# Moving cache-row copies, splitting the last factors by product and issuing three products before a norm

## The chip, the cores and the metric

The kernel runs on one core of a Trainium2 chip. The time is device microseconds (us) of one launch; the median of several runs is compared. A core has a matrix engine (PE, with PEld loading its weights), two elementwise engines (DVE and ACT), POOL, whose queue here issues DMAs and a few small operations, and SP, which issues DMAs only. All DMAs of the core run on the same 16 DMA engines: those that SP issues stand in queue q1, those that POOL issues in queue q0.

## The reference

One layer of a decoder for a prompt of 512 tokens and 8 samples of 4 tokens, 544 columns in all. What matters here is what follows the attention:

```python
y = jnp.concatenate([o_a, o_b], axis=-1) @ w_out          # h = h + y
up = rmsnorm(h, norm_ffn) @ w_up                          # 2048 -> 2 * 5504
conv = conv_b + sum(conv_w[j] * full[:, j:j + t] for j in range(3))
u, g = conv[..., :D_FF], conv[..., D_FF:]
h = h + (silu(g) * u) @ w_down
start = k_all.shape[1] - buf
return y, s_fin, k_all[:, start:], v_all[:, start:]       # the caches, shifted by 4 tokens
```

The new caches `k_s` and `v_s` are outputs: for each of the 8 samples, 1020 of the 1024 rows of 768 floats are the old rows, moved by four. That is 16 copies, 3060 KB each, from device memory to device memory. No other instruction reads or writes these rows.

## The kernel before

Activations lie feature by row, 128 features by 544 columns, each split into a high and a low part (`hi`, `lo`) so that three matmuls make one product in higher precision. A weight tile is loaded (`raw`), its high part made by ACT (`whi`, L190) and its low part by DVE (`wlo`, L191); three of each are kept.

The stages that matter, in order:

- **Output projection** (`for ot in range(KD)`, 16 output tiles). Each tile's `h` is loaded by POOL, gets the product added by DVE (L904), is stored by POOL to `hscr` (L905), squared into `acc2`, and scaled by ACT in place (L913), which waits until that store has read it.
- **Factors.** The up stage multiplies by a scheme of seven products on 2x2 blocks (in place of eight). Two tiles of `h` make one row pair `i` of four blocks b11, b12, b21, b22, from which `factors()` makes seven right-hand factors B11, B21, B22, T1 to T4, each split by `parts()` into `vh` (ACT, L875) and `vl` (DVE, L876). The first four pairs are done inside the output projection, the last four (4 to 7) when the projection has ended, pair by pair, over scratch tiles `ts` and `tu`.
- **Up stage**: 43 column pairs (`class Pair`). Pair `f` runs seven products `p1, p5, p6, p2, p7, p3, p4` of 24 matmuls each. Some of its weights are sums of two blocks: SP loads the first and POOL adds the second with an accumulating DMA (L957). Its result `a` is stored by POOL to `adr[f]` (L1085), save for three kept pairs (`KEPT`, 39 to 41), which stay on chip. After each odd `f` below 32, POOL also issues one cache copy (L1088).
- **Down stage.** First 16 products with the three kept pairs alone (24 matmuls and a 192 KB weight load each), then group 0 and group 1 of 16 pairs each and group 2 with the rest. SP fetches the pairs back from `adr` (`ar`, L1108), two buffers at a time, along with the weights (L829).

A scheduler sets the order on each engine when the program is built, from priorities (`tc.high_priority`); `tc.keep_in_program_order` pins a copy to its place among POOL's instructions. Each engine then runs its list in that order and waits on semaphores; an instruction that waits holds all that stand behind it. POOL's DMAs signal eight semaphores in turn (DMASW0 to 7). Tiles of a closed pool give their memory to the next pool, whose first user waits for the last users of the old one: so the first fetch `ar<-adr[0]` also waits for the store of the last pair, `adr[42]`.

Of the kernel before, what the change touches and what calls it, by code (L numbers as in the profile page):

```python
# [9 lines left out]
F32 = mybir.dt.float32  # L10
# [113 lines left out]
def _build(tc, nc, es, xT, st_gla, ck, cv, conv_in, vecs, w_in, w_gu, w_out, w_up, w_dn,  # L124
# [172 lines left out]
    def gps():  # L297
        return pg.tile([P, 2, 512], F32, tag="g", name="g")
# [573 lines left out]
    def parts(i, v, n, src):  # L872

        H, L = vh[i][:, v:v + n], vl[i][:, v:v + n]
        nc.scalar.activation(H, src, AF.Copy)  # L875
        nc.vector.tensor_sub(L, src, H.bitcast(F32))  # L876

    def factors(some, X, pool):
        for i in some:
            vh[i] = pool.tile([P, NV, HT], F32R, name=f"vh{i}")  # L880
            vl[i] = pool.tile([P, NV, HT], F32R, name=f"vl{i}")
            parts(i, B11, 1, X[i][:, 0, :HT].unsqueeze(1))
        for i in some:
            b11, b12, b21, b22 = X[i][:, 0, :HT], X[i][:, 0, HT:], X[i][:, 1, :HT], X[i][:, 1, HT:]
            t = HX.tile([P, 2, HT], F32, tag="ts", name="ts", bufs=1)
            u = HX.tile([P, 2, HT], F32, tag="tu", name="tu", bufs=1)
            nc.vector.tensor_sub(t[:, 0], b11, b12)
            nc.vector.scalar_tensor_tensor(t[:, 1], t[:, 0], -1.0, b22, op0=OP.mult, op1=OP.subtract)
            parts(i, T1, 2, t)
            nc.vector.tensor_sub(u[:, 0], b22, b12)  # L890
            nc.vector.scalar_tensor_tensor(u[:, 1], t[:, 1], -1.0, b21, op0=OP.mult, op1=OP.subtract)
            parts(i, T3, 2, u)
            parts(i, B21, 2, X[i][:, 1].rearrange("p (a c) -> p a c", a=2))

    X = {}
    for ot in range(KD):
        ps = gps()
        gemm(ps, [wpart(w_out, order[:8], ot * P), wpart(w_out, order[8:], ot * P)], og)
        i, j = divmod(ot, 2)
        if j == 0:  # L900
            hp = HX.tile([P, 2, NT], F32, tag="h", name="h", bufs=KD // 2 + 1 - AHEAD)
        ht = hp[:, j]
        nc.gpsimd.dma_start(ht, xT[ot * P:(ot + 1) * P, :])
        nc.vector.tensor_add(hv(ht), hv(ht), ps[:, :, :HT])  # L904
        nc.gpsimd.dma_start(hscr[ot], ht)  # L905
        if ot == 0:
            nc.scalar.activation(acc2, ht, AF.Square)
        else:
            sq = htmp("sq")
            nc.scalar.activation(sq, ht, AF.Square)  # L910
            nc.vector.tensor_add(acc2, acc2, sq)
        X[i] = hp
        nc.scalar.activation(ht, ht, AF.Copy, scale=vec[:, V_FFN + ot:V_FFN + ot + 1])  # L913
        if j == 1 and i < AHEAD:
            factors([i], X, VA)
# [27 lines left out]
    class Pair:  # L943
# [41 lines left out]
        def p2(self):  # L985
            with ahead():
                self.a12 = self.load((0, 1))
                A = wsplit(self.a12)
                nc.vector.tensor_add(self.s, self.s, self.a12)
            y = self.g[:, 1]  # L990
            product(y, A, B21)
            self.Fu, self.Fg = [FP.tile([P, FW], F32, tag="F", name="F", bufs=2) for _ in range(2)]
            for s, F in enumerate((self.Fu, self.Fg)):
                nc.gpsimd.memset(F[:, 0:2], 0.0)
                nc.scalar.activation(F[:, 2 + TP:].rearrange("p (b s) -> p b s", s=2 + TS)[:, :, 0:2],
                                     self.ci[:, s].rearrange("p (b r) -> p b r", r=2), AF.Copy, scale=(1.0, -1.0)[s])
            nc.vector.tensor_add(self.Fu[:, 2:2 + HT], y[:, :HT], self.V)

        def p7(self):
            with ahead():  # L1000
                A = wsplit(self.load((0, 0), (1, 0)))
            product(self.b0, A, T3, False)
            U3 = tmp("V")
            nc.scalar.activation(U3, self.b0[:, :HT], AF.Copy)
            second(self.Fg, self.z, U3)
            R = slice(2 + HT, FW)
            nc.vector.scalar_tensor_tensor(self.Fg[:, R], self.Fg[:, R], -1.0, rstdF[:, R], op0=OP.mult, op1=OP.mult)
# [30 lines left out]

    pairs = [Pair(f) for f in range(KF)]
    pairs[0].p1()  # L1040
    rms_stat(acc2, rstd, htmp)
    closed(hx_p)
    g0_p, G0 = opened(name="g0", bufs=NKEPT, side="right")
# [17 lines left out]
    for f, pr in enumerate(pairs):  # L1061
        if f % 4 == 0:
            n = min(4, KF - f)
            ci = FP.tile([P, 2, 4, 2 * NB], F32, tag="ci", name="ci", bufs=2)
            co = FP.tile([P, 2, 4, 2 + 2 * NB], F32, tag="co", name="co", bufs=2)
            nc.gpsimd.dma_start(ci[:, :, :n, :], ci_v[:, :, f:f + n, :])
        pr.ci, pr.co = ci[:, :, f % 4, :], co[:, :, f % 4, :]
        pr.p5()
        pr.p6()
        pr.p2()  # L1070
        pr.p7()
        if f + 1 < KF:
            pairs[f + 1].p1()
        pr.p3()
        pr.p4()
        cu, cg = pr.conv()
        nc.scalar.activation(cg[:, :FW - 2], cg[:, :FW - 2], AF.Silu)
        a = FP.tile([P, NT], F32, tag="a", name="a", bufs=1)
        nc.vector.tensor_mul(a[:, :TP], cu[:, :TP], cg[:, :TP])
        nc.vector.tensor_mul(a[:, TP:].rearrange("p (b t) -> p b t", t=TS), sv(cu), sv(cg))  # L1080
        if f in KEPT:
            kept[f] = (G0.tile([P, NT], F32R, tag="dh", name="dh"), G0.tile([P, NT], F32R, tag="dl", name="dl"))
            split(kept[f][0], kept[f][1], a)
        else:
            nc.gpsimd.dma_start(adr[f], a)  # L1085
        if f % 2 == 1 and f < 4 * NB:
            b, (src, dst) = f // 4, ((ck, k_s), (cv, v_s))[f // 2 % 2]
            tc.keep_in_program_order(nc.gpsimd.dma_start(dst[b, 0:PAST - TS, :], src[b, TS:PAST, :]))  # L1088
        if f % 4 == 3 or f == KF - 1:
            f4 = f - f % 4  # L1090
            nc.gpsimd.dma_start(co_v[:, :, f4:f + 1, :], co[:, :, :f + 1 - f4, :])
# [65 lines left out]
    for gi, ks in enumerate(groups):  # L1157
        A = {}
        with tc.high_priority(offset=min(2000, tc.cur_priority - P0)):
            for k in ks:  # L1160
                A[k] = A1[k] if k in A1 else fetch(k, where[k])
        if gi < len(groups) - 1:
            for ot in range(KD):
                ps = gps()
                gemm(ps, [wpart(w_dn, ks[i:i + 8], ot * P) for i in range(0, len(ks), 8)], A)
                nc.vector.tensor_add(hv(h[ot]), hv(h[ot]), ps[:, :, :HT])
                if gi == 0:
                    x = W3.tile([P, NT], F32, tag="hr", name="hr", bufs=1)
                    nc.sync.dma_start(x, hscr[ot])
                    nc.vector.tensor_add(h[ot], h[ot], x)  # L1170
# [113 lines left out]
```

## Time and profile before

| | us |
|---|---|
| median of 3 runs (2546.86 to 2550.66) | 2549.17 |
| the profiled execution, its own time | 2555.3 |
| its span | 2553.5 |
| PE busy (97% of the span) | 2483.1 |
| DVE busy | 1625.9 |
| ACT busy | 1063.8 |
| POOL busy | 459.4 |

The profile's page gives the busy time of each engine, the span in slices, the DMA queues, the chain of work that ended last, and groups of instructions by line. Here the chain is mostly PE, so what counts is where PE had to wait. Times in the views are counted from the start of the span. The output projection lies at about 888 to 1071 us, the up stage at 1071 to 2012, the kept products at 2012 to 2060, the groups of the down stage after that.

### The profile page before, as it was taken

How to read it: one execution, taken by the hardware profiler on the slowest of the kernel's cores; microseconds unless marked ns; L12 is line 12 of the kernel's file. 1: busy time of each engine (PE TensorE's matmuls, PEld its weight loads, DVE VectorE, ACT ScalarE, POOL GpSimd, SP SyncE). 2: the span in 40 equal slices, each digit the busy share in tenths (PEclk: the TensorE clock that was granted, in tenths of full speed). 3: DMA queues.
4: the chain of work that ended last, by engine and by line, in shares of the span. 5: the costliest groups of instructions: out<-in, count | busy, mean ns of one | idle time of the engine just before them, and what ended most of it. 6: DMA issues, size and time to landing. Idle time of an engine off the chain costs nothing.

```text
span 2553.5 us, 47085 instructions
## 1 busy us (share of the span) xinstructions
PE 2483.1 (97%) x19479; PEld 2384.3 (93%) x19479; DVE 1625.9 (64%) x2432; ACT 1063.8 (42%) x1820; POOL 459.4 (18%) x592
## 2 busy tenths in 40 slices
PE   7999999999999999999999999999999999999997
PEld 6988887899999899999999999999999999999997
DVE  7777754267776844477777878787788643342244
ACT  5344555133334443355554545454555531131142
POOL 4333424210001320021212222222121000000001
PEclk9999999999999999999999999999999999999999
DMA  7777734532222273579999999999998474453332
GB/s 202 204 198 210 191 93 131 158 94 68 75 76 76 68 204 116 127 156 279 240 274 236 267 249 261 254 269 248 239 194 180 117 223 115 112 150 91 86 97 71
DMA packets 581591, 427.72 MB, mean 168 GB/s; under 512 B 18976, under 2 KB 553728, under 8 KB 580608
## 3 DMA queue, kind: packets, MB, share of 16 engines
q1 hardware_dynamic: 462144, 248.31, 35.4%
q0 software_dynamic: 115200, 171.02, 29.4%
q10 hardware_dynamic: 4032, 5.38, 0.6%
q8 instruction: 153, 2.51, 0.4%
q14 instruction: 62, 0.51, 0.1%
HBM read 397.40 MB, written 77.37 MB: 186 GB/s over the span
## 4 chain that ended last, share of the span: by engine, by line
PE 76%; DMA 13%; DVE 5%; issue 2%; ACT 1%; POOL 0%; DVEq 0%; ACTq 0%; SPq 0%; POOLq 0%
PE g L225 43%; PE b L931 15%; PE g L931 10%; DMA raw<-in_w_up_dram 9%; DMA q<-qscr 4%; PE s L660 1%; PE v L507 1%; PE s L555 1%; PE s L542 1%; DVE wlo L191 1%; ACT whi L190 1%; DVE pr L411 1%; PE s L778 1%; PE s L781 0%; DVE h L1215 0%
## 5 line engine op out<-in xcount | busy, mean ns | idle before, releaser
L190 ACT ACTIVATE whi<-raw 128x1024 fp32r<-128x1024 f32 (+1 forms) x345 | 355.5, 1031 | 641.8 <-PE g L225 476.1
L191 DVE TENSOR_TENSOR wlo<-raw,whi 128x1024 fp32r<-128x1024 f32 (+1 forms) x341 | 408.9, 1200 | 285.2 <-ACT whi L190 280.8
L225 PE MATMUL g<-ah,wlo 128*128 128x272 f32 x2048 | 442.6, 294 | 0.0
L225 PE MATMUL g<-al,whi 128*128 128x272 f32 x2048 | 440.5, 293 | 0.0
L225 PE MATMUL g<-ah,whi 128*128 128x272 f32 x2048 | 437.3, 292 | 2.9 <-ACT whi L190 2.0
L931 PE MATMUL b<-vh,whi 128*128 128x272 f32 x1376 | 397.6, 290 | 16.4 <-ACT whi L190 15.6
L931 PE MATMUL b<-vl,whi 128*128 128x272 f32 x1376 | 397.0, 289 | 0.0
L931 PE MATMUL b<-vh,wlo 128*128 128x272 f32 x1376 | 390.6, 289 | 0.0
L225 PEld LDWEIGHTS g<-ah,whi 128*128 128x128 f32 x2048 | 325.0, 189 | 17.4 <-issue 12.9
L225 PEld LDWEIGHTS g<-ah,wlo 128*128 128x128 f32 x2048 | 326.2, 189 | 11.5 <-issue 10.1
L225 PEld LDWEIGHTS g<-al,whi 128*128 128x128 f32 x2048 | 325.4, 189 | 12.2 <-issue 10.3
L931 PE MATMUL g<-vh,whi 128*128 128x272 f32 x1032 | 298.1, 289 | 2.9 <-ACT vh L875 2.9
L931 PE MATMUL g<-vl,whi 128*128 128x272 f32 x1032 | 299.1, 290 | 1.3 <-DVE vl L876 1.3
L931 PE MATMUL g<-vh,wlo 128*128 128x272 f32 x1032 | 296.7, 287 | 0.0
L931 PEld LDWEIGHTS b<-vh,whi 128*128 128x128 f32 x1376 | 260.9, 190 | 19.3 <-ACT whi L190 18.2
L225 PE MATMUL g<-dh,whi 128*128 128x272 f32 x1248 | 258.3, 289 | 4.3 <-ACT whi L190 2.3
L931 PEld LDWEIGHTS b<-vl,whi 128*128 128x128 f32 x1376 | 260.5, 189 | 0.0
L225 PE MATMUL g<-dh,wlo 128*128 128x272 f32 x1248 | 258.9, 289 | 0.0
L225 PE MATMUL g<-dl,whi 128*128 128x272 f32 x1248 | 258.5, 289 | 0.0
L931 PEld LDWEIGHTS b<-vh,wlo 128*128 128x128 f32 x1376 | 258.2, 189 | 0.0
L190 ACT ACTIVATE whi<-rs 128x1024 fp32r<-128x1024 f32 x129 | 136.7, 1059 | 258.3 <-PE g L931 151.0
L225 PEld LDWEIGHTS g<-dh,whi 128*128 128x128 f32 x1248 | 196.5, 189 | 5.2 <-ACT whi L190 2.9
(340 smaller groups left out, 4116.8 us busy)
## 6 DMA issues: line engine op xcount, KB each, us to landing
raw<-in_w_up_dram SPq DMA_DIRECT2D x129, 512.0 KB, 7.5
raw<-in_w_in_dram SPq DMA_DIRECT2D x96, 512.0 KB, 4.3
raw<-in_w_dn_dram SPq DMA_DIRECT2D x64, 512.0 KB, 4.0
out_k_s_dram<-in_ck_dram POOLq DMA_DIRECT2D x8, 3060.0 KB, 16.9
out_v_s_dram<-in_cv_dram POOLq DMA_DIRECT2D x8, 3060.0 KB, 17.1
ra<-in_w_up_dram SPq DMA_DIRECT2D x43, 512.0 KB, 7.8
rs<-in_w_up_dram SPq DMA_DIRECT2D x43, 512.0 KB, 3.9
rs<-in_w_up_dram POOLq DMA_DIRECT2D x43, 512.0 KB, 11.4
```

The costliest lines, as they stand in the source:

```text
L190: nc.scalar.activation(hi, src, AF.Copy)
L191: eng.tensor_sub(lo, src, hi.bitcast(F32))
L225: nc.tensor.matmul(ps[:, s, :HT], a, b[:, s * HT:(s + 1) * HT], start=(i == 0 and n == 0), stop=(i == len(todo) - 1 and n == 2))
L411: nc.vector.tensor_mul(pr, kt[:, 4:5, :].broadcast_to([P, TS, QC]), q5[:, 1:5, :])
L507: nc.tensor.matmul(psv[32 * m:32 * m + 32, :QC], lhs, rhs, start=(kt == 0), stop=(kt == 5), tile_position=(0, 32 * m))
L542: nc.tensor.matmul(psc[:, :n], q[r, qi * P:(qi + 1) * P], k[r, :n], start=True, stop=True)
L555: nc.tensor.matmul(psc[r, :P], vt[:, j * P + 64 * e:j * P + 64 * e + 64], t[:, j * P:(j + 1) * P], start=(j == 0), stop=(j == qi))
L660: nc.tensor.matmul(ps[:, c * P:(c + 1) * P], KS[:, c * P:(c + 1) * P], Q[:, :, c * 64:(c + 1) * 64], start=True, stop=True)
L778: nc.tensor.matmul(po[:, c * P:(c + 1) * P], V[:, c, e * P:(e + 1) * P], ST[:, 2 * c + e, :], start=True, stop=(c == 0))
L931: nc.tensor.matmul(b[:, :HT], a_[:, i, :], x_[i][:, v, :], start=(first and i == 0 and n == 0), stop=(i == 7 and n == 2), skip_group_check ...
```

## The change

Three things. The sixteen copies leave the up stage: a list `kept_rows` holds them, and `keep_rows()` issues one each time it is called, in the output projection when `ot % 3 == 1` (5 copies) and in groups 0 and 1 of the down stage at every second tile (the other 11). `factors()` works in place of the blocks of `h` instead of `ts` and `tu`, and for the last four pairs it goes product by product over all four, with parts of one block each. `pairs[0].p5()` and `p6()` stand ahead of the norm (`rms_stat`) beside `p1()`; and the addition `s += a12` moves from `p2` to `p7`.

```diff
     def factors(some, X, pool):
+        b = {}
         for i in some:
...
-            parts(i, B11, 1, X[i][:, 0, :HT].unsqueeze(1))
+            b[i] = X[i].rearrange("p a (b c) -> p (a b) c", c=HT)
+        late = len(some) > 1
         for i in some:
-            t = HX.tile([P, 2, HT], F32, tag="ts", name="ts", bufs=1)
...
+            parts(i, B11, 1, b[i][:, 0:1])
+        for i in some:
+            nc.vector.tensor_sub(b[i][:, 0], b[i][:, 0], b[i][:, 1])
+            parts(i, T1, 1, b[i][:, 0:1])
+        for i in some:
+            nc.vector.scalar_tensor_tensor(b[i][:, 0], b[i][:, 0], -1.0, b[i][:, 3], op0=OP.mult, op1=OP.subtract)
+            parts(i, T2, 1, b[i][:, 0:1])
...
+    kept_rows = [(b, src, dst) for b in range(NB) for src, dst in ((ck, k_s), (cv, v_s))]
+    def keep_rows():
+        if kept_rows:
+            b, src, dst = kept_rows.pop(0)
+            tc.keep_in_program_order(nc.gpsimd.dma_start(dst[b, 0:PAST - TS, :], src[b, TS:PAST, :]))
     for ot in range(KD):
+        if ot % 3 == 1:
+            keep_rows()
...
     pairs[0].p1()
+    pairs[0].p5()
+    pairs[0].p6()
     rms_stat(acc2, rstd, htmp)
...
-        if f % 2 == 1 and f < 4 * NB:
-            b, (src, dst) = f // 4, ((ck, k_s), (cv, v_s))[f // 2 % 2]
-            tc.keep_in_program_order(nc.gpsimd.dma_start(dst[b, 0:PAST - TS, :], src[b, TS:PAST, :]))
...
                 nc.vector.tensor_add(hv(h[ot]), hv(h[ot]), ps[:, :, :HT])
+                if (gi * KD + ot) % 2 == 1:
+                    keep_rows()
```

How the built programs stand: POOL, from the last pairs of the up stage to the end; before, then after. `adr_9233<-a` is the store of the last pair (42), `co` the last convolution rows.

```order
L994 MEMSET F 128x2 [waits DVE_49,Activation_49] x2
L957 DMA raw<-in_w_up_dram 128x8x128 [waits DMASW4_49,DMAHW6_49,DMASW2_49,Activation_49]
L994 MEMSET F 128x2 [waits DVE_49,Activation_49] x2
L1091 DMA out_conv_out_dram<-co 256x1x54 [waits DMASW5_49,Activation_49]
L1085 DMA adr_9233<-a 128x544 [waits DVE_49]
L1215 TENSOR_TENSOR h<-h,rstd 128x272 [waits DVE_49,DMASW0_49,PE_49,Activation_49]
```

```order
L1116 DMA out_conv_out_dram<-co 256x1x54 [waits DMASW2_49,Activation_49]
L916 DMA out_v_s_dram<-in_cv_dram 48x16320
L916 DMA out_k_s_dram<-in_ck_dram 48x16320 [waits DMASW4_49]
L916 DMA out_v_s_dram<-in_cv_dram 48x16320 [waits DMASW5_49]
L916 DMA out_k_s_dram<-in_ck_dram 48x16320 [waits DMASW6_49]
L916 DMA out_v_s_dram<-in_cv_dram 48x16320
L916 DMA out_k_s_dram<-in_ck_dram 48x16320 [waits DMASW0_49]
L916 DMA out_v_s_dram<-in_cv_dram 48x16320 [waits DMASW1_49]
L916 DMA out_k_s_dram<-in_ck_dram 48x16320 [waits DMASW2_49]
L916 DMA out_v_s_dram<-in_cv_dram 48x16320 [waits DMASW3_49]
L916 DMA out_k_s_dram<-in_ck_dram 48x16320 [waits DMASW4_49]
L916 DMA out_v_s_dram<-in_cv_dram 48x16320 [waits DMASW5_49]
L1113 DMA adr_9233<-a 128x544 [waits DMASW6_49,DVE_49]
```

The 11 copies of the down stage stand in one row between the last convolution rows and the last pair's store, which now stands behind them; between them there is no other instruction.

SP at the start of the down stage, before, then after: loads of the kept products' weights (128x3x128), and the first fetches `ar`.

```order
L829 DMA raw<-in_w_dn_dram 128x3x128 [waits DMAHW7_49,DVE_49]
L1108 DMA ar<-adr_9191 128x544 [waits DMASW5_49,DMASW6_49,DMASW1_49,DMASW7_49,PE_49,Pool_49]
L1108 DMA ar<-adr_9192 128x544
L829 DMA raw<-in_w_dn_dram 128x3x128 [waits DMAHW0_49,DVE_49]
L1108 DMA ar<-adr_9193 128x544 [waits DMAHW3_49,DVE_49]
L829 DMA raw<-in_w_dn_dram 128x3x128 [waits DMAHW1_49,DVE_49]
```

```order
L829 DMA raw<-in_w_dn_dram 128x3x128 [waits DMAHW1_49,DVE_49]
L1133 DMA ar<-adr_9191 128x544 [waits DMASW4_49,DMASW2_49,DMASW6_49,PE_49,Pool_49]
L1133 DMA ar<-adr_9192 128x544
L829 DMA raw<-in_w_dn_dram 128x3x128 [waits DMAHW2_49,DVE_49]
L829 DMA raw<-in_w_dn_dram 128x3x128 [waits DMAHW3_49,DVE_49]
L829 DMA raw<-in_w_dn_dram 128x3x128 [waits DMAHW4_49,DVE_49]
```

In both, the first `ar` waits for the store of `adr_9233` (its semaphore is DMASW6); ahead of it SP has 11 of the 16 weight loads before and 13 after, and the other loads stand behind it.

DVE after the output projection's last tile, the first factors of the late pairs (`vl_11184` and so on are four tiles, one for each pair), before, then after:

```order
L876 TENSOR_TENSOR vl_11185<-ts,vh_11184 128x544 [waits Activation_49]
L876 TENSOR_TENSOR vl_11185<-tu,vh_11184 128x544 [waits Activation_49]
L876 TENSOR_TENSOR vl_11185<-h,vh_11184 128x544 [waits Activation_49]
L876 TENSOR_TENSOR vl_11189<-h,vh_11188 128x544 [waits Activation_49]
L876 TENSOR_TENSOR vl_11193<-h,vh_11192 128x544 [waits Activation_49]
L887 TENSOR_TENSOR ts<-h 128x272 [waits DVE_49]
```

```order
L876 TENSOR_TENSOR vl_11190<-h,vh_11189 128x272 [waits Activation_49]
L889 TENSOR_TENSOR h<-h 128x272 [waits DVE_49]
L876 TENSOR_TENSOR vl_11192<-h,vh_11191 128x272 [waits Activation_49]
L889 TENSOR_TENSOR h<-h 128x272 [waits DVE_49]
L876 TENSOR_TENSOR vl_11194<-h,vh_11193 128x272 [waits Activation_49]
L889 TENSOR_TENSOR h<-h 128x272 [waits DVE_49]
```

Parts of 544 columns became parts of 272, and the pairs alternate; no order within a pair is forced by a scratch tile.

## Rows read from the trace of the kernel before

**Rows 1.** Windows: length, busy time (instructions) PE, PEld, DVE, ACT, POOL, clock, DMA share, GB/s.

```profile
888.00:1071.00 183.00, 183.00 (x1460) 183.00 (x1459) 79.63 (x107) 62.21 (x80) 20.17 (x33) 1.00 0.51 143
1071.00:1096.50 25.50, 18.36 (x104) 15.75 (x104) 23.28 (x42) 17.07 (x32) 4.21 (x7) 0.80 0.51 121
...
1265.00:1855.00 590.00, 574.56 (x4542) 572.14 (x4543) 456.81 (x625) 293.20 (x517) 123.28 (x162) 0.99 1.07 254
```

**Rows 2.** Waits of PE at 1265 to 1855: total us, times, longest.

```profile
PE b L931 <- ACT whi L190: 15.6, 12, 2.9
```

**Rows 3.** Chain that ended last, up stage: start us, us, what; one such piece each pair.

```profile
1096.74 8.64 PE b L931 x69
...
1243.84 8.64 PE b L931 x69
...
1265.88 8.95 PE b L931 x69
...
1854.42 8.64 PE b L931 x69
...
1980.50 8.64 PE b L931 x69
```

**Rows 4.** DMA queues at 1237 to 1243, inside one copy: packets, MB, share.

```profile
q0 software_dynamic: 32, 2.09, 97.8%
q1 hardware_dynamic: 31, 0.02, 0.9%
```

**Rows 5.** The load of ra that SP issued at 1232.4, just before that copy's packets.

```profile
DMA to landing us min/median/max: 19.1/19.1/19.1
```

**Rows 6.** The loads of ra at 1890 to 1940, with no copy near.

```profile
DMA to landing us min/median/max: 7.5/8.9/10.4
```

**Rows 7.** The accumulating load rs that POOL issued at 1230.7, just behind that copy.

```profile
DMA to landing us min/median/max: 21.1/21.1/21.1
```

**Rows 8.** The page's DMA issues: the same load over the whole run.

```profile
rs<-in_w_up_dram POOLq DMA_DIRECT2D x43, 512.0 KB, 11.4
```

**Rows 9.** DVE in order of time, late factors: start us, us, instruction.

```profile
1072.37 1.23 DVE L191 TENSOR_TENSOR wlo<-rs,whi 128x1024 fp32r<-128x1024 f32 x1
...
1080.57 1.22 DVE L191 TENSOR_TENSOR wlo<-raw,whi 128x1024 fp32r<-128x1024 f32 x1
1081.71 0.72 DVE L876 TENSOR_TENSOR vl<-h,vh 128x544 fp32r<-128x544 f32 x1
1082.34 0.43 DVE L888 SCALAR_TENSOR_TENSOR ts<-ts,h 128x272 f32<-128x272 f32 x1
1082.70 0.43 DVE L169 SCALAR_TENSOR_TENSOR rs<-v,rs 128x272 f32<-128x272 f32 x1
...
1091.61 0.72 DVE L876 TENSOR_TENSOR vl<-tu,vh 128x544 fp32r<-128x544 f32 x1
```

**Rows 10.** PE in order of time: first matmul of pair 0 and first of its p7.

```profile
1071.33 0.28 PE L931 MATMUL b<-vh,whi 128*128 128x272 f32 x1
...
1096.58 0.29 PE L931 MATMUL b<-vh,whi 128*128 128x272 f32 x1
```

**Rows 11.** POOL in order of time at the end of the up stage.

```profile
2014.94 0.72 POOL L1091 DMA_DIRECT2D out_conv_out_dram<-co  x1 [13.65 <-ACT co L1029]
2020.70 0.60 POOL L1085 DMA_DIRECT2D adr<-a  x1 [5.04 <-DVE a L1080]
```

**Rows 12.** SP's queue in order of time, same place.

```profile
1997.16 26.80 SPq L829 DMA_DIRECT2D raw<-in_w_dn_dram  x11
2024.18 0.82 SPq L1108 DMA_DIRECT2D ar<-adr  x2
```

**Rows 13.** DMA issues at 1997 to 2024: KB each, us to landing.

```profile
adr<-a POOLq DMA_DIRECT2D x1, 272.0 KB, 2.6
```

**Rows 14.** Chain that ended last, 1995 to 2065: kept products, then group 0.

```profile
2011.81 10.56 PE g L225 x84
...
2059.83 5.17 PE g L225 x27
```

More of the change, by code (lines that the diff above doesn't have):

```diff
@@ L881, in factors @@
             vl[i] = pool.tile([P, NV, HT], F32R, name=f"vl{i}")
-            parts(i, B11, 1, X[i][:, 0, :HT].unsqueeze(1))
+            b[i] = X[i].rearrange("p a (b c) -> p (a b) c", c=HT)
+        late = len(some) > 1
         for i in some:
-            b11, b12, b21, b22 = X[i][:, 0, :HT], X[i][:, 0, HT:], X[i][:, 1, :HT], X[i][:, 1, HT:]
-            t = HX.tile([P, 2, HT], F32, tag="ts", name="ts", bufs=1)
[L886 to L893, printed above, removed]
+            parts(i, B11, 1, b[i][:, 0:1])
[5 more added lines that the diff above has]
+            parts(i, T2, 1, b[i][:, 0:1])
+        for i in some:
+            parts(i, B21, 1 if late else 2, b[i][:, 2:3] if late else b[i][:, 2:4])
+        for i in some:
+            nc.vector.tensor_sub(b[i][:, 1], b[i][:, 3], b[i][:, 1])
+            if late:
+                parts(i, T3, 1, b[i][:, 1:2])
+        if late:
+            for i in some:
+                parts(i, B22, 1, b[i][:, 3:4])
+        for i in some:
+            nc.vector.scalar_tensor_tensor(b[i][:, 2], b[i][:, 0], -1.0, b[i][:, 2], op0=OP.mult, op1=OP.subtract)
+            if late:
+                parts(i, T4, 1, b[i][:, 2:3])
+            else:
+                parts(i, T3, 2, b[i][:, 1:3])
+    kept_rows = [(b, src, dst) for b in range(NB) for src, dst in ((ck, k_s), (cv, v_s))]
[3 more added lines that the diff above has]
+            tc.keep_in_program_order(nc.gpsimd.dma_start(dst[b, 0:PAST - TS, :], src[b, TS:PAST, :]))
     X = {}
     for ot in range(KD):
+        if ot % 3 == 1:
+            keep_rows()
         ps = gps()
@@ L988, in p2 @@
                 A = wsplit(self.a12)
-                nc.vector.tensor_add(self.s, self.s, self.a12)
             y = self.g[:, 1]
@@ L1000, in p7 @@
             with ahead():
+                nc.vector.tensor_add(self.s, self.s, self.a12)
                 A = wsplit(self.load((0, 0), (1, 0)))
@@ L1067, in _build @@
         pr.ci, pr.co = ci[:, :, f % 4, :], co[:, :, f % 4, :]
-        pr.p5()
-        pr.p6()
+        if f:
+            pr.p5()
+            pr.p6()
         pr.p2()
```

## The prediction

> **What bounds the kernel now.** I read the windows by stage first. In the output projection PE is busy for the whole 183.00 us with the DMA engines at 0.51 [rows 1]: nothing is to be won there, and there is room for transfers. Two stretches lose time, and a third is short. (1) At the start of the up stage, 1071 to 1096.5, PE is busy 18.36 of 25.50 us at a granted clock of 0.80. (2) At 1265 to 1855 PE is busy 574.56 of 590 us, at clock 0.99, with the DMA engines full (1.07). (3) Between the up stage and group 0, 2011.81 to 2059.83, lie 48 us for the kept products [rows 14]. The waits of stretch 2 are of one kind, PE for a weight that ACT has yet to split, 15.6 us in 12 waits [rows 2]; the weight is late because its load is. The chain shows the price per pair: from 1096.74 to 1243.84 seven pairs take 21.01 us each, and so do the six from 1854.42 to 1980.50 [rows 3].
>
> What a cache copy does to the loads is seen inside one. From 1237 to 1243 POOL's queue q0 had 32 packets with 2.09 MB, 97.8% of the 16 engines, and SP's queue q1 31 packets with 0.02 MB [rows 4]. So the queues took turns packet by packet, but a copy's packet has 65 KB and lasts 0.978 x 6 x 16 / 32 = 2.93 us, a load's some 0.5 KB. SP's load of `ra`, waiting all that time, took 19.1 us [rows 5] against 7.5 to 10.4 without a copy [rows 6]. While a copy runs, loads stand still.
>
> **The change part by part.**
>
> *Copies out of the up stage.* From 1243.84 to 1854.42 are 28 pairs (the one from 1243.84 to 1265.88 and 27 more) in 610.58 us; at 21.01 they would take 588.3. The copies cost 22.2 us [rows 3]. Pairs without copies, at both ends, lose nothing, and the accumulating loads were there all the same; so I take all of it, **-22**. Bounds: -11 (half of it, if the accumulating loads alone run late in some pairs) and -23.
>
> *Five copies in the output projection.* They stand 36 us apart (three tiles), each behind a store of `h`; the next store comes a tile (12 us) later. One copy holds the loads for some 9 us (3 packets per engine x 2.93, since 3060 KB in 65 KB packets are 48, on 16 engines). SP loads a weight three tiles ahead of its use, with PE at 100% and the engines at 0.51 [rows 1]. This cover hides them: **0**. Without it a copy would cost what it cost in the up stage, 22.2 / 16 = 1.4 us, so 0 to +7.
>
> *Factors and three products ahead of the norm.* DVE sets this stretch: from 1072.37 on it has hardly a gap, and its last late factor starts at 1091.61 [rows 9]. PE starts pair 0 at 1071.33 and its p7 at 1096.58 [rows 10]; the 25.25 us hold four products, 96 matmuls of 0.125 (21.01 / 168), 12.0 us, and four matmuls of the norm. The parts of 544 cost 0.63 us each on DVE (1081.71 to 1082.34), those of 272 0.36 (1082.34 to 1082.70) [rows 9], so splitting them costs, and after the change more weights stand in between. DVE's list from `wlo<-rs` to the last late factor is now: 28 low parts and 16 differences of 272 at 0.36, 15.8 us; four weights at 1.14 (1080.57 to 1081.71), 4.6; the addition to `rs`, 1.1; `acc`, 0.6; three steps of the norm, 1.1. That is 23.2 us, to 1095.6, later than the 1092.3 of before. But the last four parts (T4) are wanted last; those of T2, which p6 needs, end at some 1093, and PE has its 96 matmuls out then, about 3 us sooner, after which pair 1's p1 waits for its weight. I take **-2**. Bounds: -12 (all that is lost there: 25.25 - 12.0 - 1.5), if the products really follow each other without a wait, and +3, if DVE's longer list is what decides.
>
> *Eleven copies at the end of the up stage.* In the source they are spread over two groups of the down stage. In the order they are not: POOL has no other work there, a copy depends on nothing, so POOL issues all 11 in one row as soon as the last convolution rows are out, at 2014.94 + 0.7 [rows 11], and the store of the last pair, issued at 2020.70 before, stands behind them. Copies 9 to 11 and the store wait for a semaphore of one eight DMAs earlier, which ends well before their turn. The 11 take 33 packets per engine x 2.93 = 97 us (or 34.5 MB at the 2.09 MB in 6 us: 99) [rows 4]. Starting about 2 us after the issue, at 2017.7, they end near 2115, and the store lands 2.6 us later [rows 13], at 2117 against 2023.3. Who waits for it: SP's first fetch `ar`, which needs the memory of the closed pools; it came at 2024.18, right after that landing [rows 12, 11, 13]. Behind that fetch stand all later weight loads and fetches on SP. PE has what is loaded: some seven of the 16 kept products (3.0 us each, 84 matmuls in 10.56 us) [rows 14], until about 2033, since the loads in the queue stand still as in [rows 4, 5]. Then it idles for about 80 us. So SP's list, and with it group 0, moves by 2117 - 2023.3 = **+94**. Bounds: nothing faster than 97 us is seen, since the engines are at 97.8% inside a copy; I allow -4 for the guess of the start. Upwards, at the 254 GB/s that all queues together moved in stretch 2 [rows 1], the 34.5 MB would take 136 us, +39; I stay by [rows 4], which are inside a copy, and allow a tenth more (an estimate) for gaps between one copy and the next. So +90 to +104, and +133 at the far end.
>
> *What is late next.* Before, 35.6 us passed from the first fetch to group 0's first matmuls at 2059.83 [rows 12, 14], filled with 11 fetches and 12 kept products (36 us). After the burst eight or nine kept products are left, 27 us, and the fetches set the pace. I take **-4**, bounds -9 (the fetches at two thirds of their old pace each) and 0.
>
> *Moved addition* `s += a12`: the same DVE instruction one product later, in a stage where DVE is busy 457 of 590 us [rows 1]; nothing.
>
> **Sum:** -22 - 2 + 0 + 94 - 4 = +66. The profiled execution took 2555.3 us (span 2553.5), 6 over the median of the three runs; the difference is put on the median: 2549.2 + 66 = **2615**.
>
> A rule bears on the packets. The rows show the queues alternating one load packet of 0.5 KB for one copy packet [rows 4]. The Trainium skill, page "DMA: Bandwidth & Descriptors", section "Queues, rings and completion order", says that an engine goes round the queues packet by packet and that a packet holds typically 9 to 17 descriptors. By that a load would get 9 to 17 times what the rows show, and the kept products' 13 loads would get through; the first fetch would still wait for the store, so the sum would stay within 5 us, at about 2619.
>
> **The rivals.**
>
> *A, the forecast:* 2615; its own range is 2597 to 2635. Chance 0.72.
>
> *B, loads get through beside the copies* (many copies behind each other are served otherwise than one). PE then runs the 13 kept products whose loads stand ahead of the fetch, 39 us, and idles only from about 2051. But the fetch still waits for the store, the copies last longer by what the loads take (about 5 us), and then 11 fetches remain, at the old 35.6 us or a little less: 2549 - 24 + 99 - 5 = 2619. For it: loads do flow between copies. Against it: [rows 4, 5]. Chance 0.10.
>
> *C, faster: the store does not wait for the copies' data.* If its packets passed them, or the 11 were done by about 2047, the first fetch would move by less than the 24 us gained. Priced with the fetch where it was: 2549 - 24 = 2525. Against it: the accumulating load that POOL issued just behind a copy took 21.1 us [rows 7] where 11.4 is usual [rows 8], so q0 is served in order; and 34.5 MB by 2047 would need three times the rate of [rows 4]. The same page and section of the Trainium skill says that an engine takes descriptors in the order of the ring, which agrees with those rows. Chance 0.06.
>
> *D, slower still:* the copies have gaps between them or slow each other (+104 to +133), and the up stage gives back half: 2549 - 11 + 104 = 2642 and more. This would be seen as up-stage pairs over 21.01 us. Chance 0.10.
>
> About no change: only if the burst costs what the rest gains, 0.02.
>
> **How the numbers follow.** The likeliest is A, 2615. The range runs from 2592 (2549 - 23 - 12 + 90 - 9 = 2595, and 3 for the spread of the runs) to 2640 and leaves out C and most of D. Measurement tells 0.2% (5 us) from no change. Slower by more: A, B, D, 0.92; within: 0.02; faster: 0.06.
>
> **What would show it.** Right: a gap of 70 to 90 us in PE between about 2010 and 2090 of the new span; the 11 copies landing one after another there, some 9 us apart; the first `ar` right after the landing of the last `adr`; pairs at 21.01 us from the first to the last; five copies in the output projection with PE still at 100%. The term of the factors is right if PE reaches pair 0's p7 within 21 to 25 us of its first matmul. Wrong: if the copies of the down stage land with less than 9 us between them, if the fetches come before the last copy's landing, or if loads of the kept products land within their usual time during the burst.

## The result, and the profile after

The changed kernel takes 2642.24 us (median of 4 runs, 2640.97 to 2650.4); the kernel before took 2549.56 us beside it. The ratio is 1.0369, with a 95% interval of 1.0350 to 1.0388: slower by 93 us, where 66 were forecast, and 2 us above the end of the range. The profiled execution took 2640.97 us, its span is 2638.7; against the 2553.5 of before that is +85.2. The other 7 us of the 93 come from the two profiled runs: that of before lies 6 us above its own median, that of after 1 us below.

The page shows where it is at a glance. The rows are PE's busy tenths in 40 slices (66 us each), the granted clock of TensorE, and the share of the DMA engines:

```profile
span 2638.7 us, 47129 instructions
...
PE   7999999999999999899999999999994189999997
...
PEclk9999999999999999899999999999997599999999
DMA  7777544522222676589989888898968874353331
```

Two slices with 4 and 1 tenths stand between the up stage and the down stage, and the clock falls there too. The windows of the five stretches (columns as in [rows 1]): output projection, start of the up stage, up stage proper, the burst of copies, and the catching up behind it:

```profile
885.51:1068.21 182.70, 182.70 (x1457) 182.70 (x1456) 76.99 (x107) 62.29 (x84) 22.94 (x38) 1.00 0.75 226
1068.21:1120.70 52.49, 41.27 (x272) 38.78 (x271) 39.99 (x79) 28.36 (x61) 7.49 (x10) 0.87 0.59 133
1120.70:1992.55 871.85, 871.31 (x6967) 871.09 (x6966) 697.22 (x957) 450.61 (x793) 170.93 (x222) 1.00 0.87 186
1992.55:2107.00 114.45, 20.00 (x141) 19.46 (x141) 8.29 (x16) 10.32 (x20) 6.84 (x13) 0.59 0.95 315
2107.00:2165.00 58.00, 49.13 (x343) 46.74 (x344) 23.44 (x33) 25.19 (x39) 0.00 (x0) 0.93 0.69 202
```

In the output projection PE is still busy all the time, with the DMA share up from 0.51 [rows 1] to 0.75. In the burst it is busy 20 of 114 us. The chain that ended last answers to [rows 3, 14] (start, length, what; "another core or an unknown queue" is a stretch whose releaser the profile can't name):

```profile
1120.70 8.64 PE b L956 x69
...
1961.23 8.64 PE b L956 x69
...
1992.55 15.34 PE g L225 x122
2008.53 55.68 another core or an unknown queue
2064.87 4.46 PE g L225 x18
2069.98 36.12 another core or an unknown queue
2106.76 4.46 PE g L225 x18
2113.45 4.34 DMA ar<-adr
```

From 1120.70 to 1961.23 lie 40 pairs in 840.53 us: 21.01 each, and none over. Then come 122 matmuls of the kept products (five products and two matmuls), 56 us of nothing, 18 matmuls, 36 us of nothing, 18 more, and the first fetch `ar` at 2113.45 (2024.18 before [rows 12]). The 18 matmuls took 4.46 us each time, where 24 took 3.00 in the up stage: after the gaps the granted clock is 0.50 (in the windows 2064.8 to 2070 and 2106.7 to 2111.3), the lower of its two levels, 1.2 GHz instead of 2.4.

What filled the gap are the copies. Their lines on POOL, from 1990 to 2110 (what, number, duration of the issue in ns, first and last start; then the time to landing, shortest, median and longest):

```profile
L916 POOL DMA_DIRECT2D out_v_s_dram<-in_cv_dram x6: 516/554/644, 1996.3 to 2028.8; - x6
L916 POOL DMA_DIRECT2D out_k_s_dram<-in_ck_dram x5: 505/547/601, 1996.8 to 2019.3; - x5
...
DMA to landing us min/median/max: 13.3/58.5/76.9
```

The same view of the weight loads that SP issued between 1998 and 2066:

```profile
L829 SPq DMA_DIRECT2D raw<-in_w_dn_dram x4: 367/368/368, 1998.9 to 2065.4; - x4
...
DMA to landing us min/median/max: 41.8/84.9/106.0
```

And the queues from 2010 to 2100 (packets, MB, share of 16 engines), with the last store's landing:

```profile
q0 software_dynamic: 600, 29.77, 98.3%
q1 hardware_dynamic: 603, 0.30, 1.8%
...
adr<-a POOLq DMA_DIRECT2D x1, 272.0 KB, 66.8
```

600 packets against 603: the queues took turns, one packet each, as in [rows 4], and the loads got 1% of the bytes. (Of the 600, 456 are 65 KB packets of copies, 29.77 MB; the rest are tiny.) Equal numbers alone could also come from longer turns on both sides. But from 2010.2 to 2012 each queue started 16 packets, one for each engine; from 2012 to 2013.2 neither started any; and from 2013.2 to 2015.2 each started 16 again. So a turn is one row. A weight load of a kept product has 384 rows of 0.5 KB, 24 for each engine, and 24 turns beside a packet of 3 us are 72 us, an estimate; the first took 65.3.

### The profile page after: what moved, and what is told of

It reads as the page before. It is cut to its first block, busy times and chain, and to the rows that moved or that the text cites. A ratio compares the mean times of both kernels' runs of the same rounds, so it can differ in the third digit from the quotient of the medians.

```text
span 2638.7 us, 47129 instructions
## 1 busy us (share of the span) xinstructions
PE 2482.0 (94%) x19479; PEld 2383.4 (90%) x19479; DVE 1625.7 (62%) x2448; ACT 1067.1 (40%) x1836; POOL 457.6 (17%) x592
## 4 chain that ended last, share of the span: by engine, by line
PE 81%; DMA 6%; DVE 4%; another core or an unknown queue 3%; issue 2%; ACT 1%; POOL 0%; SPq 0%; DVEq 0%; ACTq 0%; POOLq 0%
PE g L225 40%; PE b L956 19%; PE g L956 15%; DMA q<-qscr 4%; DMA ar<-adr 1%; PE s L660 1%; PE v L507 1%; PE s L555 1%; PE s L542 1%; DVE wlo L191 1%; DVE pr L411 1%; PE s L778 1%; DMA hscr<-h 1%; PE s L781 0%
## 6 DMA issues: line engine op xcount, KB each, us to landing
out_v_s_dram<-in_cv_dram POOLq DMA_DIRECT2D x8, 3060.0 KB, 40.4
```

## The experiments

The stretch ahead of PE's unbroken work in the output projection, which no kernel here means to change, ended between 884.25 and 897.19 in the profiled runs. So besides the ratio to the kernel before on the same chip (with its 95% interval), three stretches are compared by their length, read off PE's records: pair 0's seven products (from the first product's first matmul to the 169th, the norm's four not counted), the whole up stage (to the first kept product), and from there to PE's last matmul.

| kernel | ratio | pair 0 | up stage | kept products to end |
|---|---|---|---|---|
| before | 1 | 34.27 | 940.32 | 528.39 |
| after | 1.0369 (1.0350 to 1.0388) | 40.35 | 924.18 | 632.77 |
| copies only | 1.0326 (1.0302 to 1.0351) | 35.61 | 919.46 | 637.02 |
| factors only | 1.0020 (1.0005 to 1.0035) | 40.29 | 944.67 | 527.08 |
| no late copies | 0.9933 (0.9908 to 0.9959) | 39.97 | 923.80 | 527.04 |
| last store by ACT | 1.0358 (1.0338 to 1.0379) | 40.18 | 924.01 | 636.23 |
| pieces of 15 KB | 1.0471 (1.0447 to 1.0496) | 40.15 | 923.97 | 663.57 |
| pieces of 1.5 KB | 1.2806 (1.2781 to 1.2832) | 40.39 | 924.21 | 1266.76 |
| state rows early | 1.0309 (1.0292 to 1.0326) | 33.03 | 912.77 | 631.87 |
| parts of 544 | one run, 2636.67 us | 32.19 | 916.03 | 633.10 |
| copies by SP, from tile 1 | 1.0005 (0.9992 to 1.0018) | 40.43 | 924.28 | 543.61 |
| copies by SP, from tile 7, state rows early | 0.9936 (0.9922 to 0.9951) | 32.11 | 911.81 | 538.22 |
| copies by SP, from tile 7 | 0.9922 (0.9903 to 0.9940) | 32.15 | 915.98 | 530.26 |

Tiles are counted from 0. "State rows early" and "parts of 544" are explained below; the two kernels with copies from tile 7 have parts of 544.

**Which part costs what.** Two kernels with one part of the change each, and one without the eleven late copies, which leaves those rows of the outputs unwritten. The lines are against the changed kernel.

```diff
 copies only: the kernel before with its copies moved, so the old factors()
-        for i in some:
-            nc.vector.tensor_sub(b[i][:, 0], b[i][:, 0], b[i][:, 1])
-            parts(i, T1, 1, b[i][:, 0:1])
+            t = HX.tile([P, 2, HT], F32, tag="ts", name="ts", bufs=1)
...
 factors only: the changed kernel with its copies back in the up stage
+        if f % 2 == 1 and f < 4 * NB:
+            keep_rows()
...
 no late copies: the changed kernel
-                if (gi * KD + ot) % 2 == 1:
-                    keep_rows()
```

> The kernel before with the copies moved as in the change (five in the output projection, eleven in the source of the down stage); factors and norm as before. Theory (read from the trace after): the move of the copies brings -22 in the up stage and about +104 behind it, and the new factors and products ahead of the norm cost +6 where +2 less was predicted. Then this kernel is 6 us under the changed one: 2636. Rival (the 6 us at the start of the up stage come from the copies or from chance, and the factors bring the 2 us that were predicted): 2644.

> The change without its moved copies: all 16 copies are issued in the up stage as before, factors, norm and products ahead as after. Theory: from the first product of pair 0 to the first accumulating piece of pair 1 it takes 52.5 us where before took 46.4, because ACT waits for the rows of the convolution state, whose load must wait for the end of the norm; so 2549.5 + 6 = 2555.5. Rival (prediction's term, -2): 2547.5.

> The changed kernel with the eleven late copies left out (those rows of the outputs are not written); the five in the output projection stay. Theory: the boundary behind the up stage goes back to that of before, 2549.5 - 22 + 6 = 2534; 108 us under the changed kernel. Rival (part of the loss at the boundary has another cause than the copies, such as the weight loads standing ahead of the first fetch): some 7 to 15 us more, 2541 to 2549.

Measured 2639.45, 2560.66 (beside a before of 2553.42) and 2538.86 us. The table parts the terms. The changed kernel and all that keep its factors and state rows as they are take 40.0 to 40.4 us for pair 0, with or without moved copies; with the old factors it is 34.3 and 35.6. So the 6 us belong to the factors (or to the moved addition, which goes with them in these kernels), and the ratio of the factors alone, +5 us (1 to 9), agrees. The whole time of the copies-only kernel does not decide it: by the ratios it is some 11 us below the changed kernel, each with an interval of about 5 us to either side, but its profiled span is 2640.1, since its last stretch is 4 us longer, and the last stretch varies by that much (631.9 to 637.0) among the kernels with this burst. Without the late copies the last stretch is 527.04, about that of before (528.39): the 104 us there come with the eleven copies alone, 9.5 us each. With them left out 2534 was expected and 0.9933 x 2549.6 = 2532 came.

One part of the change costs nothing because it is none. With `p5()` and `p6()` of pair 0 written back behind the norm, every engine's list of instructions in the built program is the same, row for row, waits included. The planner mixes them with the norm by itself: in the trace of the kernel before, too, 54 matmuls of pair 0 stand ahead of the norm's first (49 in the changed kernel).

**What the burst holds.** Is it the store behind the copies that holds SP, or do the loads stand still by themselves?

```diff
-            nc.gpsimd.dma_start(adr[f], a)
+            (nc.scalar if f == KF - 1 else nc.gpsimd).dma_start(adr[f], a)
```

> The changed kernel with the store of the last pair (adr) issued by ACT on its own queue instead of by POOL behind the eleven copies. Theory (while copies run, all other transfers stand still, since their packets take turns with packets of 65 KB): the store lands earlier, after some 24 us (8 rows of 2 KB per engine, each after a copy's packet of 3 us), but SP's weight loads and the first fetches stand still all the same, and group 0 starts when the burst is over: 2632 to 2642, PE idle for over 80 us. Rival (only the store holds SP, and the loads would get through): the fetch comes some 60 us earlier, 2580.

Measured 2647.11, ratio 1.0358. The store's issue and landing in this kernel, from 2000 to 2112, with the first two fetches:

```profile
L1133 SPq DMA_DIRECT2D ar<-adr x2: 343/384/424, 2108.6 to 2109.0; - x2
L1113 ACTq DMA_DIRECT2D adr<-a x1: 338/338/338, 2002.4 to 2002.4; - x1
...
DMA to landing us min/median/max: 3.1/3.4/27.4
```

PE's longest wait in it, from 1990 to 2170 (total us, times, longest):

```profile
PE g L225 <- ACT whi L190: 99.2, 5, 57.4
```

The store went out at 2002.4 and landed after 27.4 us, at 2029.8; the first fetch was issued at 2108.6 all the same, 79 us later. The weight loads ahead of it in SP's list stood still by themselves. The rival falls: taking the store out of the burst gains nothing.

Then the size of a copy's packet. Two kernels cut each late copy into pieces (the lines with their numbers put in).

```diff
-            tc.keep_in_program_order(nc.gpsimd.dma_start(dst[b, 0:PAST - TS, :], src[b, TS:PAST, :]))
 pieces of 1.5 KB:
+            d, s = [t.rearrange("r (c x) -> c r x", c=2) for t in (dst[b, 0:PAST - TS, :], src[b, TS:PAST, :])]
 pieces of 15 KB:
+            d, s = [t.rearrange("(n a m) c -> a n (m c)", a=2, m=5) for t in (dst[b, 0:PAST - TS, :], src[b, TS:PAST, :])]
 both:
+            tc.keep_in_program_order(nc.gpsimd.dma_start(d, s))
```

> The changed kernel with the eleven late copies in pieces of 1536 bytes (each row of 3072 bytes in two halves) instead of 65 KB; same rows, same number of copies, same place in POOL's list. Theory (the size of a copy's packet is what keeps the loads out): weight loads issued in the burst land within some 10 to 25 us instead of 65 to 106, the kept products run on for about 39 us, and PE idles some 20 to 30 us less; the fetch still waits for the store behind the copies, so 2612 to 2630, if the copies take no longer in small pieces; if they do, by so much more. Rival (eleven copies fill the DMA engines, whatever the size of the pieces): loads stand 60 us and more as before, 2640.

> The changed kernel with the eleven late copies in pieces of 15,360 bytes instead of 65,280; same rows and places. Theory (each engine gives one turn to a load's packet of 0.5 KB and then one to a copy's packet, so a copy's packet length sets how long a load stands): a kept product's weight load has 384 rows of 0.5 KB, 24 for each engine; with turns of 3 us that made 72 us (65 measured), with turns of 0.7 us it makes 17 us. So loads issued in the burst land within 15 to 30 us, PE has four or five more kept products while the copies run and idles 10 to 15 us less: 2624 to 2634, if the burst is no longer. Rival (the loads stand because the engines are full, whatever the size of the pieces): 65 us and more again, 2640.

Measured 3272.67 and 2673.94 us: both far slower than any theory said. First the one with 15 KB. SP's weight loads issued from 2003 to 2066:

```profile
L829 SPq DMA_DIRECT2D raw<-in_w_dn_dram x6: 367/368/368, 2004.0 to 2065.6; - x6
...
DMA to landing us min/median/max: 22.1/39.8/57.2
```

The queues from 2010 to 2060, with eight copies in flight:

```profile
q0 software_dynamic: 1740, 15.99, 95.6%
q1 hardware_dynamic: 1013, 0.50, 4.3%
```

The same from 2100 to 2148, when three copies were left:

```profile
q0 software_dynamic: 860, 7.68, 37.7%
```

And PE's waits in this kernel from 1990 to 2170:

```profile
PE g L225 <- ACT h L1149: 66.9, 1, 66.9
PE g L225 <- ACT whi L190: 60.2, 6, 15.7
```

The turn-taking is confirmed. A copy packet now lasts 0.72 us, and 1041 of them stood against 1013 packets of the loads' queue in 50 us. The first load took 22 us, and the next landed 18.6, 19.6 and 17.6 us after one another (2026.16, 2044.74, 2064.38, 2082.00), against 24 x 0.72 = 17. So the loads of six kept products landed in the burst, instead of one (at 2064.22; the next three landed as it ended, from 2106.11 on). But two things ate it. The pattern's outer dimension is 2, and three copies together kept 0.377 of the 16 engines busy: two engines each (6/16 = 0.375), so the last three ran nearly 60 us on six engines and the burst ended at 2150, not 2106. (The Trainium skill, page "DMA: Bandwidth & Descriptors", section "Why a DMA increments its semaphore by 16 and not by 1", says that a transfer goes to the largest number of engines up to 16 that divides the slowest dimension of both its sides; these rows agree.) And PE then stood 66.9 us for another wait: ACT, in order, was at the split of the first fetch, 61.9 us, with its copy of a finished product behind it.

With 1.5 KB only one copy ran at a time, on two engines; the copies' lines in that kernel:

```profile
L917 POOL DMA_DIRECT2D out_v_s_dram<-in_cv_dram x6: 4787/4787/4853, 1998.9 to 2678.7; - x6
...
DMA to landing us min/median/max: 67.1/67.4/69.8
```

Eleven times 67.4 us is 741, and its last stretch is 740 us longer than without late copies. Its weight loads took 9 to 13 us, but beside 14 idle engines that says nothing on the size of packets: this run is inconclusive on what it was made for.

**Where the 6 us at the start of the up stage are.** PE's waits there in the changed kernel, from 1068 to 1125:

```profile
PE b L956 <- ACT V L1029: 5.3, 1, 5.3
PE g L956 <- DVE vl L876: 2.1, 2, 1.5
```

The convolution's state rows `ci` on ACT, and what ACT waited for there (us, times):

```profile
L1019 ACT ACTIVATE F<-ci x4: 198/201/217, 1101.4 to 1123.7; 128x16 f32<-128x16 f32 x4
...
  DMA ci<-in_conv_in_dram: 5.2, 1
```

The norm's last step on DVE (line 171), and who waited for it:

```profile
L171 DVE SCALAR_TENSOR_TENSOR rstd<-rs x2: 436/440/443, 1089.0 to 1094.2; 128x272 f32<-128x272 f32 x2
...
  POOL vcv L1078: 1.8, 1
```

PE waits for `V`, which ACT has yet to copy; ACT stands 5.2 us at `F<-ci`; those rows come late, because POOL may load `vcv` and `ci` only after the norm's last step (they take the memory of the closed pool `HX`), and that step starts at 1094.2, 26.0 us after the first product. In the kernel before it started at 1088.1, 16.8 us after the first product; the same line there:

```profile
L171 DVE SCALAR_TENSOR_TENSOR rstd<-rs x2: 434/434/435, 1084.4 to 1088.1; 128x272 f32<-128x272 f32 x2
```

Two kernels test this: one loads these rows early, into memory that is free; one has parts of 544 again.

```diff
+    vcv = RA.tile([P, NVEC - V_CW], F32, name="vcv")
+    nc.gpsimd.dma_start(vcv, vecs[:, V_CW:])
...
+    ci0 = RA.tile([P, 2, 4, 2 * NB], F32, name="ci0")
+    nc.gpsimd.dma_start(ci0, ci_v[:, :, 0:4, :])
     pairs = [Pair(f) for f in range(KF)]
...
 the other kernel, in factors():
-        late = len(some) > 1
+        late = False
```

> The changed kernel with the vectors of the convolution and the first rows of its state loaded before the norm, into memory that is free by then (in the changed kernel they go where the norm's tiles lay, so their loads wait for its last step on DVE). Theory: ACT no longer stands 5 us for these rows, and the stretch from the first product of pair 0 to the 169th matmul after it (pair 0's seven products) falls from 40.3 us to 34 or 35, as before the change had it: 2635. Rival (DVE's longer list is what is late, so another wait takes its place): 39 to 40 us, 2640.

> The changed kernel with the late factors formed in place in the new order, but in parts of 544 where the kernel before has them (two factors at a time) instead of 272. If the number of parts were the cause of the 6 us, the stretch of pair 0's seven products would go back to 35 us. Theory (the norm's last step now stands behind all parts in DVE's list, in this kernel too): 38 to 40 us; time 2640.

Measured 2634.81 and 2636.67. Loading early brings pair 0 to 33.03 us: the wait is the cause. (Among PE's waits from 1076 to 1130, `V L1029` no longer stands.) The other expectation missed: with parts of 544 pair 0 takes 32.19 us, though the norm's last step is as late as ever, 25.3 us after the first product. What differs is ACT's list in the built program (here without line and buffer numbers, and without the two copies of `rstd`):

```
changed kernel                           parts of 544
ACTIVATE F<-ci 128x8x2 x2                ACTIVATE whi<-raw 128x1024
ACTIVATE whi<-raw 128x1024               ACTIVATE V<-b 128x272
ACTIVATE V<-b 128x272                    ACTIVATE whi<-rs 128x1024
ACTIVATE whi<-rs 128x1024                ACTIVATE V<-b 128x272
ACTIVATE V<-b 128x272                    ACTIVATE F<-ci 128x8x2 x2
```

There the planner put `F<-ci` behind the two weights and the two copies of `V` that PE waits for. So the late rows alone don't cost anything; they cost where they stand ahead, in a list that is worked off in order, of what PE needs next. This kernel has the moved addition too, so that is not what cost. With parts of 544 the in-place factors are worth 34.27 - 32.19 = 2.1 us. That it is the -2 of the prediction is chance: that was reckoned for parts of 272.

**A version that keeps the gains.** The five copies in the output projection stay; the eleven are issued by SP, between its weight loads.

```diff
-    def keep_rows():
+    def keep_rows(eng=nc.gpsimd):
...
-                if (gi * KD + ot) % 2 == 1:
-                    keep_rows()
 from tile 1:
+                if (gi * KD + ot) % 2 == 1:
 from tile 7:
+                if gi * KD + ot >= 7 and (gi * KD + ot) % 2 == 1:
 both:
+                    keep_rows(nc.sync)
```

> The changed kernel with the eleven late copies issued by SP, between its weight loads of the first two groups of the down stage, one every second tile, instead of by POOL. Theory (what costs is that all eleven run at once and ahead of the last store): the boundary behind the up stage goes back to that of before and the copies hide in the groups, so 2549.5 - 22 + 6 = 2534. Rival (a copy costs the loads beside it about 1.4 us wherever it stands, as in the up stage, or more since loads on SP's own queue stand behind it): 2534 + 11 x 1.4 = 2549 or more.

> A version meant to keep the gains and drop both losses: copies in the output projection as in the change; the other eleven issued by SP among its weight loads, every second tile from the eighth tile of the first group on (so behind that group's fetches); the late factors in place in parts of 544; the vectors and the first state rows of the convolution loaded before the norm. Theory: up stage -22, its start -3 (33 where before took 34.3, less pair 1's slow start), boundary as before, copies in the groups at most 4 us for the fetches of the second group: 2549.5 - 22 - 3 + 2 = 2527. Rival (each copy on SP's own queue holds the loads behind it, wherever it stands): the 15 us seen with the copies from the second tile on come back, 2540.

> As the version before this one (eleven copies issued by SP from the eighth tile of the first group on, late factors in parts of 544), but with the convolution's vectors and first state rows loaded after the norm, where the changed kernel has them. Theory: the 6 us that the version before lost in the first kept products came from that load's new place in memory, on which the first rows of h lie (ACT's copies of h waited for the last pair's convolution); without it the boundary is that of before, the start of the up stage still takes 32 us (ACT's list has the state rows behind two weights there), and the copies in the groups cost 2 to 4 us: 2549.5 - 24 - 1 + 3 = 2527 to 2530. Rival (the 6 us come from the copies on SP): 2536 or more.

The first gave 2555.64 us, ratio 1.0005: the rival's 15 us came, but not as 1.4 us for each copy. PE's waits from 1990 to 2560 in it:

```profile
PE g L225 <- ACT dh L190: 11.7, 3, 9.7
```

One wait of 9.7 us: the copies at the second and fourth tile ran into the fetches that the first group still needs (the fetch issued at 2053.40, beside the second of them, took 14.8 us to land; the first five took 2.7 to 3.5 us). From the eighth tile on PE's waits for `dh` are 0.5 and 1.7 us in all. The second version (parts of 544, early state rows) gave 2537.99, the third (parts of 544 alone) 2534.21 us. By their ratios to the kernel before, that is 2533 and 2530 against its 2549.6: the second missed its 2527, the third met its 2527 to 2530. The largest wait of PE in the second, from 1985 to 2110:

```profile
PE g L225 <- ACT h L1151: 7.8, 7, 3.8
```

The largest in the third, from 1995 to 2110:

```profile
PE g L225 <- ACT h L1148: 2.6, 1, 2.6
```

The third's copies, from 2000 to 2500:

```profile
L916 SPq DMA_DIRECT2D out_v_s_dram<-in_cv_dram x6: 580/582/636, 2095.3 to 2338.1; - x6
...
DMA to landing us min/median/max: 12.4/13.2/14.0
```

The second lost 6 to 7 us in the first 100 matmuls of the kept products (19.2 us, 12.6 in the third), and only the place of `vcv` and `ci0` differs: ACT's list there has the copies of `h` behind the last pair's convolution and SiLU; in the third one stands ahead of both and two more ahead of the SiLU. That it is the memory of `vcv`, on which rows of `h` come to lie, that makes the planner put them so is argued, not shown. The third has the last stretch 2 us above that of before, with all eleven copies in it, and is faster than the kernel before by 0.8% (0.6 to 1.0).

## Why the prediction was wrong

The direction and the mechanism of the burst were right, the sum was too small by some 22 us (+88.3 where +66 was forecast, between the profiled runs and without the -3.1 of the unchanged stretch ahead of the output projection). Three terms made it so, by 8.1, 7.9 and 6.5 us: the factors, whose sign was wrong, the burst and the catching up. By its steps:

- *Copies out of the up stage, -22.* Right: from pair 1's piece to the first kept product 871.85 us against 2011.81 - 1117.75 = 894.06 (1117.75 is the first piece of [rows 3] and 21.01), so -22.2, with every pair at 21.01.
- *Five copies in the output projection, 0.* Right: PE busy 182.70 of 182.70 us, DMA share 0.75, and the same length in both kernels.
- *Factors and products ahead, -2 (bounds -12 and +3).* The step that failed in kind: +6.1 (52.49 us from pair 0's first matmul to pair 1's piece of the chain, which starts at its p7, against 1117.75 - 1071.33 = 46.42). The prediction looked at DVE's list and at PE's weights, and its own sign, `p7` reached within 21 to 25 us of the first product, came true (22.1 us). The loss is behind that, where PE waits 5.3 us for `V`: the norm's last step moved from 16.8 to 26.0 us after the first product, and who waits for it (POOL's loads of the state rows, then ACT's list with `V` in it) was not followed. The "three products ahead" were no change at all. The moved addition, put at nothing, was not tried by itself, but the kernel with parts of 544 has it and loses nothing here.
- *The burst, +94.* The mechanism stood, and the copies landed 9 to 10 us apart as foreseen; the size did not: the store landed at 2105.91, 113.4 us after the first kept product, against 2023.3 - 2011.81 = 11.5 before, so +101.9. The rate came from 6 us inside one copy, 2.93 us a packet [rows 4]; in the burst the mean of the 65 KB packets is 3.11 us. 33 packets for each engine are some 102 us, and from the first packet's start to the last one's end it took 107 (1997.7 to 2104.75), where 97 was reckoned. The tenth allowed for gaps covers this; why the packets are slower here stays open.
- *Catching up, -4.* Missed by 6.5: the whole loss of the stretch is 632.77 - 528.39 = 104.4, so +2.5 behind the burst. The first fetch came 7.5 us after the store's landing (2105.91 to 2113.45), since SP's weight loads ahead of it had stood still too and two were yet to be issued; PE ran its first matmuls at half the clock, and some ten of the sixteen kept products were still to do, where eight or nine were reckoned.

Of the rivals, B (loads get through) fell by the rows: four loads in the burst, 42 to 106 us each. In the 15 KB kernel, where they partly did, ACT's list held PE at the first fetch, which was seen nowhere in the prediction. The rule of the Trainium skill on which B drew (page "DMA: Bandwidth & Descriptors", section "Queues, rings and completion order": an engine drains a packet of some 9 to 17 descriptors before it goes on) is not what this trace shows: 603 load packets carried 0.30 MB, one row of 0.5 KB each, and 16 of them, one for each engine, stood between two rounds of copy packets. C fell: the store landed after the last copy. D had the size of the burst with what follows it (104), but its other half, an up stage that gives back only 11, did not come; that its 2642 was measured is luck, met by other misses.

The range's lower end, 2592, was summed from the terms' own ends; the upper one, 2640, was not. The upper ends that the prediction gave (-11, +7, +3, +104 and 0) add up to 2652, which holds the result. The factor term's end, +3, was worked out for DVE alone, and was passed by 3.

## What to carry to other kernels

A transfer that depends on nothing is issued as soon as its queue is free, wherever the source has it: what holds it back must be a queue with other work in it (here SP, among its loads), and beside it loads in small pieces get one packet for each of its packets, with pieces of 65 KB as with 15 KB. When one engine's steps move, follow who waits for the last of them through the loads to the lists of the other engines: a late row costs only what stands behind it in an in-order list. And look at the built order before counting an edit: a line moved in the source may move nothing.

## What was not expected of the hardware

The 65 KB packets of a copy took, as a mean over each copy, 2.70 to 2.83 us in the up stage of the kernel before, 3.02 to 3.31 us in the burst, and 2.68 to 3.16 us in the output projection of the changed kernel; what makes the difference was not tried and stays open. A copy whose pattern has an outer dimension of 2 ran on 2 of the 16 engines (0.377 for three). The kernels with the early state rows took 20.91 us a pair instead of 21.01 (runs of 24 matmuls took 2.98 instead of 3.00 us); this is 4 us over the up stage and has no explanation here.
